# Three conditioning visits begun one block earlier, in buffers taken from the shared ring

## The chip, the core and the metric

The kernel runs on one core of a Trainium2 chip. The metric is the device time of one launch in microseconds. TensorE (PE in the profile) multiplies, ScalarE (ACT) and VectorE (DVE) work element by element, GpSimd (POOL) does small jobs, and SyncE's queue (SP) issues nearly all loads. Each engine runs its own instructions in the order in which they were compiled, and waits for others through semaphores.

## What is computed

One layer of a hybrid decoder for two request groups at once, 256 prompt tokens and 8 x 4 sample tokens, so that every matrix product has 288 columns. Cut to what matters here:

```python
mod = silu(c) @ w_ada + b_ada                      # six parts: sh1, sc1, g1, sh2, sc2, g2, 2048 wide each
h = rmsnorm(x, norm1) * (1 + sc1) + sh1
u_pool, z, xbc, dt = split(h @ w_in)               # 512, 1536, 2560, 24 columns
mix = concat([pool_mixer(u_pool), ssd_mixer(z, xbc, dt)]) @ w_out
x = x + g1 * mix
h2 = rmsnorm(x, norm2) * (1 + sc2) + sh2
up = h2 @ w_up                                     # then a short conv and silu on the gate half
x = x + g2 * (act @ w_down)                        # and a last rmsnorm
```

Parts 0 and 1 of `mod` (sh1, sc1) are needed before `w_in`; parts 2 and 3 (g1, sh2) only after `w_out`. The change concerns when the products for parts 2 and 3 are made.

## The kernel before, in words

All weights come once from DRAM, as one long stream cut into pieces of 128 partitions x up to 1024 columns of fp32 (512 KB), loaded into SBUF by `load` (line 267). A weight piece is split into a rounded high part (ACT, `whi`, line 289) and the rest (DVE, `wlo`, line 291), and each 128x128 tile of it gives three matmuls of 288 columns (`mm3`, lines 303 to 305). The conditioning weights are not split: a piece is the moving operand of matmuls whose stationary operand is `sc_c`, the conditioning vectors (line 372, `adag`, for parts 0 and 1; line 405, `adap`, for the others).

**Blocks.** The x/B/C columns of `w_in` and some others (28 column tiles) are made in seven blocks over groups of rows k (`BLOCKS`, line 45). The blocks numbered 4, 5 and 6 each take all 28 column tiles over four row tiles: k 4 to 7, 8 to 11, 12 to 15. A column tile over four rows is one unit of 12 matmuls; a piece holds two units. The loop at line 1046 runs over blocks, and inside over units `i`. While a block runs, the conditioning for the next rows is made in *group visits* (`next(nxt)`): a visit reads four pieces of parts 0 and 1, and after a group's last visit the next rows are modulated. The list `VIS` (line 48) says behind which units the visits stand: in block 5 behind units 3, 9, 15 and 20.

**The ring.** Pieces for blocks 0 to 5 and for the group visits share a ring of 16 buffers (`_W`, line 494): four tagged `raw` and four tagged `rawa` in the pool `w1`, eight tagged `raw` in the pool `w0`. `_need_order` (line 89) sorts the pieces by an assumed time of need, and `top_up` (line 277) issues them while fewer than 16 (`RAW0 + RAW1 + RAWA`) lie between the next load and the oldest one not yet fetched. Six pieces are loaded before, then 103 in this order, so the last has the number 108.

**Part visits.** Parts 2 and 3 are made by the generator `adas = ada_visits((2, 3), AK)` (lines 412 and 959): 16 visits. Each loads four pieces into the four `rawa` buffers (one step), lets two more steps pass, and in the fourth step runs its matmuls, the last loaded piece first, held at their place in program order. The pieces of the following visit go into the same four buffers, so they are loaded once the matmuls have read them. All 16 visits take 65 steps. Before the change, block 6 (the last) begins with closing `w0`, moving the four `rawa` buffers out of the shared ring, the `dt` product, the small loads of `late_states`, and one step of `adas` (line 1069). Then each unit of block 6 pulls 4 x 5.01/28 = 0.716 step, and each unit of the gate stretch 4 x 11.01/62 = 0.710 step.

**Gate stretch.** After block 6 come eight more column tiles of `w_in` (`uz_units`, line 943: six of z, the gate of the mixer, and two of the pool), 64 units of six matmuls. Between them runs `back` (line 1033), the convolution and the state-space part, which has small matmuls in the midst of ACT and DVE work. At its end `drain(adas)` (line 1105) finishes what visits are left.

The order of each engine's instructions is fixed by a scheduler at compile time: it goes by program order as priority, but may put an instruction whose buffer is free ahead of an earlier one that still waits. Matmuls of the visits keep their place.

Of the kernel before, what the change touches and what calls it, by code (L numbers as in the profile page):

```python
# [39 lines left out]
RAW0, RAW1, RAWA, RAW2 = 8, 4, 4, 4  # L40
# [4 lines left out]
BLOCKS = [((0, 1), (0, 28)), ((1, 1), (0, 16)), ((1, 3), (16, 28)), ((2, 2), (0, 16)),  # L45
          ((4, 4), (0, 28)), ((8, 4), (0, 28)), ((12, 4), (0, 28))]

VIS = ([14], [1, 9], [2, 6, 10], [4], [3, 9, 15, 20], [3, 9, 15, 20], [])
TP = 0.4
TV, TL = 2.0, 2.8  # L50
GB = 4
VA = (5.01 / 28, 11.01 / 62)
AK, AY, ADA_OUT = 2, 2, 4

RB1, RB2, RB3 = 1.0, 1.0, 1.0
# [26 lines left out]
def _xbc_chunks(bi):  # L82
    (k0, gk), (a, b) = BLOCKS[bi]
    mper = RAWC // (gk * P)
    cuts = [a, *([4, 8] if bi == 0 else []), *range(a + (12 if bi == 0 else mper), b, mper), b]
    return [(list(range(k0, k0 + gk)), list(range(m, n))) for m, n in zip(cuts, cuts[1:])]


def _need_order():

    visits = iter([(gi, q) for gi in range(1, len(KGROUPS))
                   for q in range(0, KT * 256 * KGROUPS[gi][1] // RAWC, AQ[gi])])
    t, need = 0.0, []
    for bi, ((_, gk), (a, b)) in enumerate(BLOCKS[:-1]):
        chunks = {ms[0]: ci for ci, (_, ms) in enumerate(_xbc_chunks(bi))}
        for i, m in enumerate(range(a, b)):
            if m in chunks and (bi or chunks[m] > 1):
                need.append((t - TL, ("xbc", bi, chunks[m])))
            t += TP * gk
            if i in VIS[bi]:  # L100
                gi, q = next(visits)
                need += [(t, ("ada", gi, q + j)) for j in range(AQ[gi])]
                t += TV
    assert next(visits, None) is None
    return [key for _, key in sorted(need, key=lambda e: e[0])]
# [59 lines left out]
def kernel(ctx: ExitStack, tc, ins, outs):  # L165
# [99 lines left out]
    wp = [None]  # L265

    def load(key, ring="raw"):
        off, cols = S.items[key]
        t = wp[0].tile([P, RAWC], F32, tag=ring, name="raw_" + "_".join(map(str, key)))
        nc.sync.dma_start(t[:, :cols], wflat[off:off + P * cols].rearrange("(p n) -> p n", p=P))  # L270
        return t

    queue = deque(_need_order())
    ahead = {}
    nloads = [0]

    def top_up():

        while queue and nloads[0] - min((n for n, _ in ahead.values()), default=nloads[0]) < RAW0 + RAW1 + RAWA:
            key = queue.popleft()  # L280
            ahead[key] = (nloads[0], load(key))
            nloads[0] += 1

    def fetch(key):
        return ahead.pop(key)[1]
# [7 lines left out]
    def split(raw, a, n, name, urgent=True, pin=False):  # L293
        with tc.high_priority() if urgent else nullcontext():
            cast, (hi, lo, rest) = split_steps(raw, a, n, name)
        if pin:
            tc.keep_in_program_order(cast)
            tc.keep_in_program_order(rest)
        return hi, lo
# [112 lines left out]
    def ada_visits(parts, step):  # L412

        plan = [(part, k0) for part in parts for k0 in range(0, KT, step)]
        ahead, end = [], None

        def chunks(v):
            part, k0 = plan[v]
            for k in range(k0, k0 + step):
                for h in range(2):  # L420
                    ahead.append((k, h, load(("adap", part, k, h), "rawa")))
            for _ in range(3):
                yield

        yield from chunks(0)
        for v, (part, k0) in enumerate(plan):
            if end:
                ada_end(*end)
                end = None
            if k0 == 0:  # L430
                ps = pa.tile([P, 512], F32, tag="ada", name=f"adap{part}")
            whole(ps, ahead, step, True)
            ahead.clear()
            if k0 + step == KT:
                end = part, ada_sb(ps, 512, f"p{part}")
            yield
            if v + 1 < len(plan):
                yield from chunks(v + 1)
        ada_end(*end)
        yield  # L440
# [137 lines left out]
    def late_loads():  # L578
        nc.vector.tensor_copy(selr, seli)
        nc.vector.tensor_scalar(csr, vec[:, K_TRI:K_TRI + N], 0.0, None, ALU.mult)  # L580

    def late_states():
        nc.sync.dma_start(poolw, ins["pool_w"])
        n = XT * NB * 3
        st = sx[0].tile([P, n + 4 * NB * 15], F32, name="st")
        nc.sync.dma_start(st, ins["st"])
        stc.append(st[:, 0:n].rearrange("p (g m b l) -> p g m b l", g=4, m=5, b=NB))
        nc.gpsimd.tensor_copy(ups.rearrange("p m b l -> p (m b) l")[:, :, 0:15],
                              st[:, n:].rearrange("p (m l) -> p m l", l=15))
# [353 lines left out]
    def uz_units(m):  # L943
        for ps in project_units(("uz", m), KT, order=MIXK if m == ULATE[-1] else None):
            yield
        if m < 4:
            nc.scalar.copy(upp[:, m, 15:15 + NP], ps[:, 0:NP])
            nc.scalar.copy(ups[:, m, :, 15:19], samp(ps[:, NP:N]))
        else:
            g, t = divmod(m - 4, 3)  # L950
            nc.scalar.activation(zy_of(g)[:, t, :], ps[:, :N], AF.Silu)
            zdone.add((g, t))
# [6 lines left out]
    adas = ada_visits((2, 3), AK)  # L959
# [78 lines left out]
    def pull(gn, rate):  # L1038

        credit[id(gn)] = credit.get(id(gn), 0.0) + rate  # L1040
        while credit[id(gn)] >= 1:
            credit[id(gn)] -= 1
            next(gn, None)

    nloads[0] = len(first) + KT // 4
    for bi in range(len(BLOCKS)):
        last = bi + 1 == len(BLOCKS)
        top_up()
        if last:

            wp[0].drop(w0)
            wp[0].move("rawa", "raw", "rawa")
            w0_ctx.close()
            sx[0] = mx_ctx.enter_context(tc.tile_pool(name="sx", bufs=1, reuse_waits="tile"))
            wp[0].add(sx[0], "raw", "raw", 1)
            raw = load(("dt",))[:, :KT * NH].rearrange("p (k h) -> p k h", h=NH)
            wdt = wp[0].tile([P, RAWC], F32R, tag="whi", name="whi_dt")
            with tc.high_priority():
                nc.gpsimd.memset(wdt.bitcast(F32), 0.0)
                both = wdt[:, :DTW * KT].rearrange("p (k c) -> p k c", c=DTW)  # L1060
                nc.scalar.copy(both[:, :, 0:NH], raw)
                nc.vector.tensor_tensor(both[:, :, 32:32 + NH], raw, both[:, :, 0:NH].bitcast(F32), ALU.subtract)
            ps = pm.tile([P, 512], F32, tag="mm", name="mm_dt")
            for k in range(KT):
                w = wdt[:, DTW * k:DTW * k + P]
                nc.tensor.matmul(ps[:, :N], w, xhi[0][k], start=k == 0, stop=False)
                nc.tensor.matmul(ps[:, :N], w, xlo[0][k], start=False, stop=k == KT - 1)
            late_states()
            next(adas)
            dt_stage(ps)  # L1070
        elif bi == 4:
            nc.sync.dma_start(vec, ins["vec"])
        elif bi == 5:
            late_loads()
        for i, m in enumerate(xbc_units(bi)):
            if not last:
                top_up()
                if bi == 0 and i in (3, 7, 13):
                    ci = {3: 2, 7: 3, 13: 4}[i]
                    ready["xbc", 0, ci] = split(fetch(("xbc", 0, ci)), 0, len(_xbc_chunks(0)[ci][1]) * P,  # L1080
                                                f"xbc0_{ci}", pin=True)
                if i in VIS[bi]:
                    next(nxt)
                    top_up()
            else:
                pull(back, 0.5 if m < 20 else RB1) if m >= 9 else None
                pull(adas, 4 * VA[0])

    late = {}
    n = 0  # L1090
    zlast = 3 * (4 - ZEARLY) * KT // YK
    for m in list(range(4 + 3 * ZEARLY, 16)) + ULATE:
        for _ in uz_units(m):
            n += 1
            for gn in late.values():
                pull(gn, 0.5)
            pull(adas, 4 * VA[1])
            pull(back, RB2 if n <= zlast else RB3)
            if n == zlast:
                drain(back)  # L1100
                back = ssd3
        if m < 4:
            late[m] = pool_units(m)
            next(late[m])
    drain(adas)
    wp[0].move("rawa", "rawa", "raw")
    adas = ada_part_units(4, AY)
# [36 lines left out]
    for i in range(KT // YK):  # L1144
# [6 lines left out]
        if i == 3:  # L1151
            psq = aux("ysum")
            col_sums(psq, ssq, ones[:, 0:1], True, True)
            _, rstdy = rstd_of(psq, NH * 64, "rstdy")
# [209 lines left out]
    rstdf, _ = rstd_of(psf, D, "rstdf", False)  # L1364
# [151 lines left out]
```

## Time and profile before

| what | value |
|---|---|
| median of three runs | 1350.02 us (1346.77 to 1351.32) |
| the profiled execution's own time | 1346.89 us |
| its span, first to last instruction | 1345.1 us |
| granted TensorE clock | 0.998 |
| PE busy | 1329.6 us (99%) |
| DVE, ACT, POOL busy | 824.6, 578.6, 222.3 us |
| block 5 | about 133 to 185 us |
| dt and block 6 | about 185 to 252 us |
| gate stretch | about 252 to 364 us |

The profiled execution took 1346.89 us, of which its span holds 1345.1 us; 1.8 us lie around it. It is 3.1 us under the median of the runs. The profile has 512 records of `adap` matmuls in all, 256 of them for the 16 visits of parts 2 and 3, so 16 records stand for one visit. In the tables of stretches the columns are: stretch, its length, busy time of PE, PEld (weight loads), DVE, ACT and POOL (number of instructions), granted clock, busy share of the DMA engines, GB/s. In the timelines they are: start, length, engine, line, operation, output and inputs, shapes, count, and in brackets the idle time before it and what ended that.

### The profile page before, as it was taken

Reading aid. Unit: us, or ns where it says so; the run is one execution under the profiler, and the core shown is the slowest. Engines: PE = TensorE matmul, PEld = TensorE weight load, DVE = VectorE, ACT = ScalarE, POOL = GpSimd, SP = SyncE. Lnnn points to the kernel's source line nnn. Section 1 sums busy time; section 2 is a strip of 40 time slices with the busy share of each in tenths; the row PEclk is TensorE's granted clock in tenths of the full one; section 3 lists DMA queues with packets and bytes.
Section 4 is the critical chain, followed back from the end, with each engine's and each line's share of the span. In section 5 each row is a group of like instructions: output and inputs, shape, how many; then the busy total and the mean of one; then the engine's idle time right before and its main releaser. Section 6 shows DMA issues by size and latency. Waiting matters only on the chain.

```text
span 1345.1 us, 26211 instructions
## 1 busy us (share of the span) xinstructions
PE 1329.6 (99%) x10517; PEld 1245.2 (93%) x10517; DVE 824.6 (61%) x1382; ACT 578.6 (43%) x911; POOL 222.3 (17%) x449
## 2 busy tenths in 40 slices
PE   9999999999999999999999999999999999999997
PEld 7889998876789889989999999999999999999997
DVE  5675569878765468555565445665655556666543
ACT  5343245677733335433443333433433334444442
POOL 0000012123122123100221001221210021122221
PEclk9999999999999999999999999999999999999999
DMA  9999678888898886777455445555545555555521
GB/s 373 405 408 370 232 263 309 316 298 318 299 395 325 311 322 226 270 268 260 171 193 176 166 175 189 198 191 194 182 162 170 189 194 191 191 191 196 184 72 71
DMA packets 97482, 323.19 MB, mean 240 GB/s; under 512 B 10768, under 2 KB 19920, under 8 KB 97360
## 3 DMA queue, kind: packets, MB, share of 16 engines
q1 hardware_dynamic: 93600, 310.79, 63.9%
q0 software_dynamic: 3184, 9.69, 2.0%
q8 instruction: 82, 1.34, 0.4%
q10 hardware_dynamic: 576, 1.03, 0.2%
q14 instruction: 40, 0.33, 0.1%
HBM read 309.78 MB, written 10.39 MB: 238 GB/s over the span
## 4 chain that ended last, share of the span: by engine, by line
PE 93%; DMA 2%; DVE 2%; issue 2%; ACT 0%; POOL 0%; SPq 0%; DVEq 0%; POOLq 0%; ACTq 0%
PE mm_down L304 7%; PE mm_down L303 7%; PE mm_down L305 7%; PE mm_val L304 6%; PE mm_gate L303 6%; PE mm_gate L304 6%; PE mm_gate L305 6%; PE mm_val L305 6%; PE mm_val L303 6%; PE xbc L303 4%; PE xbc L304 4%; PE xbc L305 4%; PE adap L405 4%; PE adag L372 2%; PE mm_out L303 2%; PE mm_out L304 2%
## 5 line engine op out<-in xcount | busy, mean ns | idle before, releaser
L304 PE MATMUL mm_down<-al,whi_down 128*128 128x288 f32 x688 | 202.5, 294 | 0.0
L303 PE MATMUL mm_down<-ah,whi_down 128*128 128x288 f32 x688 | 202.4, 294 | 0.0
L305 PE MATMUL mm_down<-ah,wlo_down 128*128 128x288 f32 x688 | 202.0, 294 | 0.0
L304 PE MATMUL mm_val<-h2l,whi_val 128*128 128x288 f32 x640 | 189.1, 296 | 0.0
L304 PE MATMUL mm_gate<-h2l,whi_gate 128*128 128x288 f32 x640 | 189.0, 295 | 0.0
L303 PE MATMUL mm_gate<-h2h,whi_gate 128*128 128x288 f32 x640 | 188.7, 295 | 0.0
L305 PE MATMUL mm_val<-h2h,wlo_val 128*128 128x288 f32 x640 | 188.4, 294 | 0.0
L305 PE MATMUL mm_gate<-h2h,wlo_gate 128*128 128x288 f32 x640 | 188.3, 294 | 0.0
L303 PE MATMUL mm_val<-h2h,whi_val 128*128 128x288 f32 x640 | 187.9, 294 | 0.0
L291 DVE TENSOR_TENSOR wlo_gate<-raw_gate,whi_gate 128x1024 fp32r<-128x1024 f32 x80 | 99.1, 1238 | 135.6 <-ACT whi_gate L289 135.6
L291 DVE TENSOR_TENSOR wlo_down<-raw_down,whi_down 128x1024 fp32r<-128x1024 f32 x96 | 108.0, 1125 | 116.6 <-ACT whi_down L289 116.6
L289 ACT CAST whi_down<-raw_down 128x1024 fp32r<-128x1024 f32 x96 | 92.4, 962 | 167.1 <-PE mm_down L304 119.3
L289 ACT CAST whi_gate<-raw_gate 128x1024 fp32r<-128x1024 f32 x80 | 84.0, 1051 | 159.5 <-PE mm_gate L304 78.1
L289 ACT CAST whi_val<-raw_val 128x1024 fp32r<-128x1024 f32 x80 | 84.1, 1051 | 127.4 <-issue 111.4
L303 PE MATMUL xbc<-h1h,whi_xbc 128*128 128x288 f32 x448 | 133.5, 301 | 0.8 <-ACT h1h L490 0.7
L304 PE MATMUL xbc<-h1l,whi_xbc 128*128 128x288 f32 x448 | 132.3, 296 | 0.0
L305 PE MATMUL xbc<-h1h,wlo_xbc 128*128 128x288 f32 x448 | 130.1, 295 | 0.0
L303 PEld LDWEIGHTS mm_down<-ah,whi_down 128*128 128x128 f32 x688 | 129.2, 188 | 0.0
L304 PEld LDWEIGHTS mm_down<-al,whi_down 128*128 128x128 f32 x688 | 129.1, 188 | 0.0
L305 PEld LDWEIGHTS mm_down<-ah,wlo_down 128*128 128x128 f32 x688 | 129.0, 188 | 0.0
L303 PEld LDWEIGHTS mm_gate<-h2h,whi_gate 128*128 128x128 f32 x640 | 120.3, 188 | 5.0 <-ACT ah L1279 3.4
L305 PEld LDWEIGHTS mm_gate<-h2h,wlo_gate 128*128 128x128 f32 x640 | 120.5, 188 | 0.0
(331 smaller groups left out, 2979.1 us busy)
## 6 DMA issues: line engine op xcount, KB each, us to landing
raw_adap<-wflat SPq DMA_DIRECT2D x128, 512.0 KB, 6.4
raw_gate<-wflat SPq DMA_DIRECT2D x80, 512.0 KB, 3.6
raw_val<-wflat SPq DMA_DIRECT2D x80, 512.0 KB, 3.5
raw_ada<-wflat SPq DMA_DIRECT2D x64, 512.0 KB, 9.6
raw_xbc<-wflat SPq DMA_DIRECT2D x50, 512.0 KB, 9.5
raw_down<-wflat SPq DMA_DIRECT2D x48, 512.0 KB, 3.4
raw_out<-wflat SPq DMA_DIRECT2D x32, 512.0 KB, 7.3
raw_down<-wflat SPq DMA_DIRECT2D x32, 384.0 KB, 3.4
```

The lines of the kernel that those rows point to most:

```text
L289: yield nc.scalar.copy(hi[:, :n], raw[:, a:a + n])
L291: yield hi, lo, nc.vector.tensor_tensor(lo[:, :n], raw[:, a:a + n], hi[:, :n].bitcast(F32), ALU.subtract)
L303: nc.tensor.matmul(ps, whi[:, w], bh, start=first, stop=False)
L304: nc.tensor.matmul(ps, whi[:, w], bl, start=False, stop=False)
L305: nc.tensor.matmul(ps, wlo[:, w], bh, start=False, stop=last)
L372: i = nc.tensor.matmul(ps[32 * j:32 * j + 32, :nb], sc_c[:, ck, :], raw[:, c:c + nb], start=q0 + n == 0, stop=q0 + AQ[gi] >= nq and n + 1 ...
L405: i = nc.tensor.matmul(ps[32 * j:32 * j + 32, :], sc_c[:, k, :], raw[:, 512 * (j % 2):512 * (j % 2) + 512], start=k == step - 1, stop=k == ...
```

## The change

- The group visits of block 5 stand behind units 1, 5, 9 and 13 (before: 3, 9, 15 and 20). The order of need changes with them.
- At unit 14 of block 5 the four `rawa` buffers leave the shared ring, and the limit in `top_up` falls from 16 to 12. From unit 14 to unit 27 each unit makes one whole step of `adas`: 14 steps, which hold visits 0, 1 and 2 and the loads of visit 3. Their matmuls stand behind units 17, 21 and 25.
- The single step of `adas` ahead of `dt_stage` in block 6 is gone, and so is the move of the buffers there.
- Block 6 pulls 4 x 4.01/28 = 0.573 step a unit (16 steps: visits 3 to 6, and the loads of visit 7), and the gate stretch 4 x 8.76/62 = 0.565 step (35 are left: visits 7 to 15). Before, it was 5 visits in block 6 and 11 in the gate stretch.

```diff
-VIS = ([14], [1, 9], [2, 6, 10], [4], [3, 9, 15, 20], [3, 9, 15, 20], [])
+VIS = ([14], [1, 9], [2, 6, 10], [4], [3, 9, 15, 20], [1, 5, 9, 13], [])
...
-VA = (5.01 / 28, 11.01 / 62)
+VA = (14, 4.01 / 28, 8.76 / 62)
...
+    room = [RAW0 + RAW1 + RAWA]
...
-        while queue and nloads[0] - min((n for n, _ in ahead.values()), default=nloads[0]) < RAW0 + RAW1 + RAWA:
+        while queue and nloads[0] - min((n for n, _ in ahead.values()), default=nloads[0]) < room[0]:
...
             wp[0].drop(w0)
-            wp[0].move("rawa", "raw", "rawa")
             w0_ctx.close()
...
             late_states()
-            next(adas)
             dt_stage(ps)
...
                 if i in VIS[bi]:
                     next(nxt)
                     top_up()
+                if bi == len(BLOCKS) - 2 and i >= VA[0]:
+                    if i == VA[0]:
+                        room[0] -= RAWA
+                        wp[0].move("rawa", "raw", "rawa")
+                    next(adas)
             else:
                 pull(back, 0.5 if m < 20 else RB1) if m >= 9 else None
-                pull(adas, 4 * VA[0])
+                pull(adas, 4 * VA[1])
...
-            pull(adas, 4 * VA[1])
+            pull(adas, 4 * VA[2])
             pull(back, RB2 if n <= zlast else RB3)
```

## The prediction

> **What bounds the kernel now.** I read the page's head first, to see which engine is full.
>
> ```profile
> span 1345.1 us, 26211 instructions
> PE 1329.6 (99%) x10517; PEld 1245.2 (93%) x10517; DVE 824.6 (61%) x1382; ACT 578.6 (43%) x911; POOL 222.3 (17%) x449
> PE 93%; DMA 2%; DVE 2%; issue 2%; ACT 0%; POOL 0%; SPq 0%; DVEq 0%; POOLq 0%; ACTq 0%
> ```
>
> PE is idle for 1345.1 - 1329.6 = 15.5 us in all, and 93% of the chain that ended last is PE. The change neither adds nor removes a matmul, so only idle time of PE can move. The second view is the table of stretches for block 6 and for the gate stretch, the third the waits of PE from block 6 into the output stage.
>
> ```profile
> 185.30:252.40 67.10, 67.04 (x514) 56.87 (x512) 58.28 (x134) 30.24 (x43) 15.43 (x29) 1.00 0.79 289
> 252.40:364.00 111.60, 109.60 (x918) 82.76 (x915) 86.48 (x160) 89.09 (x199) 23.25 (x35) 1.00 0.85 310
> ...
> PE adap L405 <- DMA raw_adap<-wflat: 0.7, 1, 0.7
> PE pool L939 <- DVE pout L933: 0.6, 1, 0.6
> PE y L871 <- DVE e L859: 0.6, 2, 0.4
> ```
>
> Block 6 has 0.06 us of PE idle time, the gate stretch 111.60 - 109.60 = 2.00 us: 0.7 for a part visit whose pieces came late, 1.2 for results of DVE. That is the whole room for a gain in these stretches. A verdict of faster or slower needs more than 0.3%, or 4.05 us (about what a measurement of this kernel can tell from no change; the three runs alone lie 4.55 us apart). Block 5 must now carry three visits more. Its timetable comes from the group visits in it:
>
> ```profile
> 139.20 1.93 PE L372 MATMUL adag<-raw_ada,sc_c 128*32 128x256 f32 x32
> 150.78 1.93 PE L372 MATMUL adag<-raw_ada,sc_c 128*32 128x256 f32 x32
> 162.37 1.93 PE L372 MATMUL adag<-raw_ada,sc_c 128*32 128x256 f32 x32
> 172.37 1.93 PE L372 MATMUL adag<-raw_ada,sc_c 128*32 128x256 f32 x32
> ```
>
> Between the second and the third lie six units (11.59 us), between the third and the fourth five (10.00): a unit takes 1.59 us, a visit 11.59 - 6 x 1.59 = 2.05. Four units stand ahead of the first, so the block began at 139.20 - 4 x 1.59 = 132.84.
>
> **The group visits moved forward.** Behind units 1, 5, 9 and 13 they begin at 132.84 + 2 x 1.59 = 136.02, then every 4 x 1.59 + 2.05 = 8.41 us: 144.43, 152.84, 161.25. Are their pieces there? I follow the order of need through the ring: the four visits read loads 81 to 84, 87 to 90, 93 to 96 and 99 to 102 (before: 82 to 85, 89 to 92, 96 to 99, 102 to 105). A load goes out when the one 16 places earlier has been read.
>
> ```profile
> 111.02 1.75 SPq L270 DMA_DIRECT2D raw_ada<-wflat  x4
> ...
> 120.58 2.49 SPq L270 DMA_DIRECT2D raw_ada<-wflat  x4
> ...
> DMA to landing us min/median/max: 8.6/10.5/10.5
> ```
>
> Places 66 to 68 and 72 to 74, read by the last two group visits of block 4, come free where these two rows stand: 111 and 120.6. The longest landing of group pieces that I found, 10.5 us (third row, those issued at 92 to 98, while DMA was full), gives 123 and 134, with 136.02 and 144.43 as the needs. The later two wait for pieces read by about 136 and 138, so they land by 149, against 152.84 and 161.25. Nothing waits, and I cost this at nothing; its cover is some 10 us in each case. The last modulation comes 11 us sooner and stands beside matmuls, as before.
>
> **The four buffers and the limit.** Followed through `top_up`, load 108 goes out behind unit 10, before and after; at unit 14 the queue is empty, so the lower limit never acts. And SP shows that the four buffers already served part visits there:
>
> ```profile
> 151.48 1.28 SPq L270 DMA_DIRECT2D raw_xbc<-wflat  x3
> 163.07 0.33 SPq L270 DMA_DIRECT2D raw_dt<-wflat  x1
> 163.45 0.42 SPq L583 DMA_DIRECT2D poolw<-pool_w  x1
> 163.97 1.04 SPq L270 DMA_DIRECT2D raw_adap<-wflat  x2
> 165.11 1.13 SPq L270 DMA_DIRECT2D raw_xbc<-wflat  x2
> 173.93 0.80 SPq L270 DMA_DIRECT2D raw_adap<-wflat  x2
> 174.79 0.42 SPq L270 DMA_DIRECT2D raw_xbc<-wflat  x1
> 175.26 0.96 SPq L759 DMA_DIRECT2D h<-h  x2
> ```
>
> Visit 0 was loaded at 164 to 174, in block 5, though its matmuls came later. Cost of this part: 0. What is new on SP is that 12 more loads (visits 1 to 3) may stand ahead of block 6's pieces and the state loads `h`. The scheduler let block 6's loads pass waiting ones here (rows 165.11 against 173.93), and their buffers now come free with the group visit at 152.84, 10 us sooner than that of the `dt` row at 163.07. I cost it at 0 for block 6; POOL's queue is not passed by anything.
>
> **Three part visits in block 5.** This is the term that decides. Visit 0 stands four units behind the last group visit, visits 1 and 2 four units behind the one before, so each begins 8.41 us after the start of the visit that frees its buffers: 169.66, 178.07, 186.48. How soon can four pieces be there?
>
> ```profile
> 346.36 1.92 PE L405 MATMUL adap<-raw_adap,sc_c 128*32 128x512 f32 x16
> ...
> L270 SPq DMA_DIRECT2D raw_adap<-wflat x4: 328/368/422, 347.5 to 348.8; - x4
> DMA to landing us min/median/max: 3.5/5.8/8.2
> ...
> 357.02 1.92 PE L405 MATMUL adap<-raw_adap,sc_c 128*32 128x512 f32 x16
> ...
> L270 SPq DMA_DIRECT2D raw_adap<-wflat x4: 328/369/422, 358.1 to 359.4; - x4
> DMA to landing us min/median/max: 3.8/5.0/6.3
> ...
> 367.07 1.92 PE L405 MATMUL adap<-raw_adap,sc_c 128*32 128x512 f32 x16
> ```
>
> The visit at 357.02 had its next pieces issued from 358.1 to 359.4 with little beside them; the last landed at most 6.3 us after its issue, at 365.7, which is 8.7 us after the visit began. The one at 346.36, with other weights in the queue, got its last at 348.8 + 8.2 = 357.0, or 10.65 us after. Against 8.41 a visit in block 5 is 0.3 us late in the first case and 2.25 in the second. Before, visits stood some 10 us apart. The last loaded piece is read first, so lateness goes straight into PE, and the unit behind it waits too.
>
> Which row is nearest? These rows say how full DMA is:
>
> ```profile
> 100.00:110.00 10.00, 10.00 (x84) 9.66 (x87) 4.31 (x11) 2.67 (x3) 0.00 (x0) 1.00 1.03 410
> ...
> 152.00:162.00 10.00, 10.00 (x86) 9.50 (x78) 5.61 (x8) 2.10 (x2) 0.00 (x0) 1.00 0.64 235
> 162.00:172.00 10.00, 10.00 (x94) 8.91 (x93) 4.80 (x8) 3.15 (x3) 0.00 (x0) 1.00 0.70 244
> ```
>
> At 410 GB/s a visit's 2.10 MB take 5.1 us of each 8.41, which leaves 3.3 us, or 1.35 MB, for others. In the way come two `h` loads (1.18 MB), released earlier by the modulation, and a piece or two of block 6 (0.52 MB each): enough to delay one visit of three. So visits 0 and 2 at 0.3 each and visit 1 half-way, at 1.3: +1.9 us. Ends: 0 (block 5 has no PE idle time to give back) and 3 x 2.25 = 6.75.
>
> The Trainium skill, page "DMA: Bandwidth & Descriptors", section "Anatomy of one DMA — SWDGE (gpsimd) path", gives a DMA about 2.0 us plus its bytes over 436 GB/s. That is a fit for GpSimd's path; as an estimate, 2.10 MB would then be there 6.8 us after the first issue, 7.9 after the visit's start, no visit would be late, and the sum would be 1.9 us less. The trace's 358.1 to 365.7 is 7.6 us, so the measurement speaks for lateness; this is rival C.
>
> **Block 6 and the gate stretch.** Block 6 gets 4 visits for 5, the gate stretch 9 for 11. Visits in the gate stretch now stand 4/0.565 = 7.1 units apart in place of 5.6, so (367.07 - 357.02 - 2.05) x 7.1/5.6 + 2.05 = 12.2 us, more than the 10.65 above: the 0.7 us wait for pieces goes. What is late next is DVE, because visits are PE work behind which DVE catches up:
>
> ```profile
> 230.00:240.00 10.00, 10.00 (x80) 8.40 (x79) 9.95 (x23) 4.92 (x5) 4.07 (x6) 1.00 0.83 296
> 240.00:250.00 10.00, 10.00 (x74) 7.87 (x73) 9.90 (x18) 4.26 (x6) 3.58 (x5) 1.00 0.69 261
> ...
> 331.94 1.58 DVE pp L922
> ...
> 360.79 1.14 DVE wlo_out L291
> ```
>
> DVE is full in 230 to 250, yet block 6 as a whole needs 58.28 us of it in 67.10 - 2.05 = 65.05, so its backlog runs off behind it. In the gate stretch the chain of waits goes through DVE around these two rows, at 324 to 337 and 357 to 363, some 20 us. PE's cover thins there by 2 x 2.05 / 111.6 = 3.7%, or 0.7 us. Ends: -1.2 (those waits vanish) and +4.1 (all of the cover becomes waiting).
>
> **Sum.** +1.9 - 0.7 + 0.7 = +1.9 us. Against the profiled execution's 1346.89 that is 1348.8; against the median, 3.1 us higher, 1352.
>
> **The rivals.**
>
> *A, slower: every one of the three visits comes late.* If the `h` loads, `st` and block 6's pieces fall in the queue ahead of each of them, as at 346.36, block 5 loses 6.75 us; with -0.7 and +0.7 that is 1356.8. For it: four loads of 512 KB and others share one queue, and the spacing of 8.41 is below every start-to-landing time above. Against it: DMA was only 0.64 to 0.70 busy in 152 to 172. It decides from a mean lateness of 4.05/3 = 1.35 us.
>
> *B, slower: DVE takes over in the gate stretch.* All of the 4.1 us of cover becomes waiting: 1.9 - 0.7 + 4.1 = 5.3, or 1355.3. For it: 58.28 of 67.10 us in block 6, then 86.48 of 111.6. Against it: PE waited 1.2 us for DVE in all.
>
> *C, a little faster: the visits in block 5 are hidden.* If the buffers' older readers let the first loads out sooner, nothing is late there; the 0.7 goes, and half of the DVE waits at best: -1.3, or 1348.7. For it: only 0.3 us is missing. Even with all 2.0 us of idle time gone it isn't 0.3%.
>
> That the buffers' move does nothing by itself is part of the sum already.
>
> **How the numbers follow.** Forecast 0.45, A 0.25, B 0.10, C 0.20. The range runs from C with its last waits gone (1350.02 - 2.0 = 1348.0, and 1 us for the scatter of the runs) to A and 1 us more: 1347 to 1358. The likeliest case alone: 1350 to 1354. Slower by over 0.3%: A and B, 0.35. Faster: no mechanism, only the scatter of the medians, 0.06. Within: 0.59.
>
> **What would show it.** In the changed kernel: group visits about 136, 144, 153 and 161; `adap` visits about 170, 178 and 186, with PE waits on `raw_adap` of 0 to 2 us each (A: 2 and more, C: none); `mm_dt` some 6 us later than before; no wait for `raw_adap` in the gate stretch; its length near 107.5 us, and waits on DVE near 2 us (B: 4 or more). The prediction is wrong if block 6's first pieces land late behind the visits' loads on SP, if group visits wait for their pieces, or if the gate stretch doesn't shrink by the two visits.

## The result, and the profile after

| | before | after |
|---|---|---|
| median, 11 runs each on one chip | 1348.19 us (1346.77 to 1351.32) | 1351.43 us (1350.69 to 1354.11) |
| ratio, 95% interval | 1 | 1.0026 (1.0018 to 1.0033) |
| profiled execution, its span | 1346.89, 1345.1 us | 1351.43, 1349.7 us |

The change costs 0.26% of 1348.19, or 3.5 us (the two medians lie 3.2 us apart). That is inside the 0.3% that I called a measurement's limit, and with eleven runs on each side it is clearly above zero. The forecast was +1.9 us. The two profiled executions, which the rest compares, lie 4.6 us apart in span: that of before is 1.3 us under the median of its runs, that of after stands on its own. So differences of about a microsecond between two profiles can be scatter.

The head of the page of the changed kernel, for comparison with the three lines of before:

```profile
span 1349.7 us, 26220 instructions
PE 1331.4 (99%) x10517; PEld 1246.2 (92%) x10517; DVE 822.4 (61%) x1382; ACT 581.9 (43%) x913; POOL 221.5 (16%) x449
PE 94%; DVE 2%; DMA 2%; ACT 1%; issue 1%; POOL 0%; SPq 0%; DVEq 0%; POOLq 0%
```

The same 10517 matmuls, and PE still fills 99%. Its idle time went from 15.5 us to 1349.7 - 1331.4 = 18.3. To place the 4.6 us I cut both executions at the same events (first matmul of `mm_dt`, `uz`, `mm_out` and `mm_up`). First the stretches of before, cut at these events (dt with block 6, the gate stretch, and the output stage up to the first matmul of `mm_up`), in the columns of the prediction's tables:

```profile
185.70:252.40 66.70, 66.64 (x511) 56.47 (x509) 58.28 (x134) 30.24 (x43) 15.43 (x29) 1.00 0.80 290
252.40:362.40 110.00, 108.09 (x910) 81.59 (x907) 84.88 (x155) 87.49 (x195) 23.25 (x35) 1.00 0.84 309
362.40:493.60 131.20, 130.73 (x997) 111.76 (x995) 74.15 (x146) 46.08 (x67) 30.08 (x57) 1.00 0.88 334
```

And the same view of the kernel after: dt with block 6, the gate stretch, the output stage.

```profile
189.90:258.40 68.50, 66.91 (x510) 56.41 (x508) 57.74 (x132) 30.66 (x43) 11.50 (x27) 1.00 0.85 323
258.40:367.70 109.30, 107.01 (x894) 81.73 (x891) 82.38 (x157) 89.80 (x197) 25.90 (x38) 1.00 0.79 290
367.70:499.30 131.60, 129.22 (x981) 111.41 (x979) 77.48 (x149) 47.84 (x67) 32.01 (x57) 1.00 0.85 322
```

| stretch | part visits, before to after | length before | length after | difference |
|---|---|---|---|---|
| start to `mm_dt` | 0 to 2 | 185.7 | 189.9 | +4.2 |
| dt and block 6 | 5 to 5 | 66.7 | 68.5 | +1.8 |
| gate stretch | 10 to 9 | 110.0 | 109.3 | -0.7 |
| output stage | 1 to 0 | 131.2 | 131.6 | +0.4 |
| from `mm_up` to the end | | 851.5 | 850.4 | -1.1 |

Read the table by its second column, which counts where the visits were found. Before, the sixteenth visit stood in the output stage (at 367.07), so the gate stretch held ten and not the eleven named ahead of the prediction. Two visits of 2.05 us went ahead of `mm_dt`, which is 4.1 us late for it. One visit each left the gate stretch and the output stage, which should have become 2.05 us shorter each. The last cut falls into the waits for `h2h`, 1.2 us in both kernels: before, 0.8 us of them lie behind the cut, after, none. With these 0.8 us put on one side, the last two differences are -0.4 and -0.3. So the two stretches gave back 0.7 and 0.4 us of 2.05 each: the work was paid for in front and hardly given back behind. From `mm_dt` to the end it is 1159.4 us before and 1159.8 after, with two visits less.

A part of the reason is in the waits of PE from block 5 to the output stage of the kernel after (us in total, times, longest):

```profile
PE xbc L304 <- DVE cvp L712: 1.6, 2, 1.3
...
PE pool L940 <- DVE pout L934: 1.1, 2, 0.9
PE cse L852 <- DVE yo L838: 1.0, 1, 1.0
PE mm_out L304 <- ACT whi_out L290: 1.0, 2, 0.8
PE y L872 <- DVE e L860: 0.3, 1, 0.3
```

No wait on `raw_adap` is left in this stretch, and none for the pieces of the moved visits. All that is there is PE waiting for results of DVE and ACT: 5.0 us, where before had 0.6 + 0.6 for DVE and 0.7 for pieces. With the waits at `mm_up`, PE's idle time from 130 to 520 us grew from 3.27 to 6.25 us, +3.0. The rest of the 4.6 us lies in PE's busy time (1329.6 to 1331.4 with the same matmuls), which no run here takes apart. In the gate stretch it is the larger part: PE's idle time grew by 0.4 us there, while its busy time fell by 1.1 us for a visit of 1.9. How far one pair of profiles carries is seen from the first experiment below: its kernel is as fast as before, and its profile has 4.62 us of idle time in the same window.

Where the visits came to stand is in the timeline of PE of the kernel after (start, length, ..., count):

```profile
136.15 1.93 PE L373 MATMUL adag<-raw_ada,sc_c 128*32 128x256 f32 x32
...
161.39 1.93 PE L373 MATMUL adag<-raw_ada,sc_c 128*32 128x256 f32 x32
...
175.70 1.93 PE L406 MATMUL adap<-raw_adap,sc_c 128*32 128x512 f32 x16
...
185.18 1.92 PE L406 MATMUL adap<-raw_adap,sc_c 128*32 128x512 f32 x16
...
189.92 0.29 PE L1066 MATMUL mm_dt<-h1h,whi_dt 128*128 128x288 f32 x1
...
194.92 1.92 PE L406 MATMUL adap<-raw_adap,sc_c 128*32 128x512 f32 x16
```

The four group visits stand within 0.2 us of the predicted places. The part visits do not: not at 169.66, 178.07 and 186.48, but at 175.70, 185.18, and 194.92, the third behind `mm_dt`. Nothing waits in front of them. In the compiled order of PE the first of them stands 7.6 units behind the last group visit, where the program has it 4 behind, and the third 0.4 units behind `mm_dt`. So the scheduler deferred them at compile time; that matmuls of the visits keep their place, as the text ahead of the prediction has it, does not hold against the matmuls around them. It also shifted the later ones: in units of 12 matmuls behind `mm_dt`, the visits of block 6 and the next stand at 5, 10, 16, 21, 27 before and at 0.4, 4.4, 11, 18, 25 after. SyncE's queue in the kernel after shows when pieces were asked for:

```profile
162.09 1.75 SPq L270 DMA_DIRECT2D raw_adap<-wflat  x4
163.89 0.49 SPq L270 DMA_DIRECT2D raw_dt<-wflat  x1
...
176.79 1.75 SPq L270 DMA_DIRECT2D raw_adap<-wflat  x4
...
186.28 1.75 SPq L270 DMA_DIRECT2D raw_adap<-wflat  x4
...
221.57 1.64 SPq L760 DMA_DIRECT2D h<-h  x3
```

The second and third sets of four go out 1.1 us after the start of the visit that frees the buffers, and the visits stand 9.48 and 9.74 us apart: between the 8.7 and the 10.65 that the prediction had measured from start to landing, and more than the 8.41 of the program's order. The `h` loads, which the prediction put in the way of the second visit, go out at 221.57 and later, so they stood in the way of none; before, the first two went out at 175.26. PE waits for none of them in either kernel.

### The profile page after: what moved, and what is told of

Read it like the earlier page. It is cut to its first block, busy times and chain, and to the rows that moved or that the text cites. A ratio compares the mean times of both kernels' runs of the same rounds, so it can differ in the third digit from the quotient of the medians.

```text
span 1349.7 us, 26220 instructions
## 1 busy us (share of the span) xinstructions
PE 1331.4 (99%) x10517; PEld 1246.2 (92%) x10517; DVE 822.4 (61%) x1382; ACT 581.9 (43%) x913; POOL 221.5 (16%) x449
## 4 chain that ended last, share of the span: by engine, by line
PE 94%; DVE 2%; DMA 2%; ACT 1%; issue 1%; POOL 0%; SPq 0%; DVEq 0%; POOLq 0%
PE mm_down L305 7%; PE mm_down L304 7%; PE mm_down L306 7%; PE mm_val L305 6%; PE mm_gate L304 6%; PE mm_gate L305 6%; PE mm_gate L306 6%; PE mm_val L306 6%; PE mm_val L304 6%; PE xbc L304 4%; PE xbc L305 4%; PE xbc L306 4%; PE adap L406 4%; PE adag L373 2%; PE mm_out L304 2%; PE mm_out L305 2%
## 5 line engine op out<-in xcount | busy, mean ns | idle before, releaser
L292 DVE TENSOR_TENSOR wlo_down<-raw_down,whi_down 128x1024 fp32r<-128x1024 f32 x96 | 107.5, 1120 | 116.8 <-ACT whi_down L290 116.6
```

What stands on the lines that cost most here:

```text
L292: yield hi, lo, nc.vector.tensor_tensor(lo[:, :n], raw[:, a:a + n], hi[:, :n].bitcast(F32), ALU.subtract)
```

## The experiments

These accounts of the 3.5 us were tried, and the letters stand in the expectations (S was put down last, behind the run with denser visits):

- **T, thinned cover.** Visits are PE work behind which DVE and ACT catch up. Behind `mm_dt` they cost almost nothing, ahead of it their full 2 us.
- **P, the place in block 6.** The loss is the 1.3 us wait behind the reciprocal of `dt`, which a visit no longer covers.
- **G, the group visits** moved forward cost by themselves.
- **F, full price.** PE work counts in full wherever it stands, so that the loss has some other cause.
- **S, a matter of which visits.** Only certain ones are cover, and others would give their time back.

Two more letters stand in the expectations. L says that block 6's own pieces come late; but the kernel after has no wait of PE for a weight split of block 6, only the two for `cvp` above. D says that DVE time as such is missing beside the reciprocal.

### The group visits alone

```diff
-VIS = ([14], [1, 9], [2, 6, 10], [4], [3, 9, 15, 20], [3, 9, 15, 20], [])
+VIS = ([14], [1, 9], [2, 6, 10], [4], [3, 9, 15, 20], [1, 5, 9, 13], [])
```

> The kernel before with the group visits of block 5 behind units 1, 5, 9 and 13 and nothing else of the change. Theory P (the loss of 0.26% comes from where the part visits now stand in block 6 and later, measured against DVE work): 1.000 of before, within 0.05%; block 5 keeps its length of about 52.8 us. Rival G (the early group visits cost something themselves, through pieces that come late or a modulation that falls into the splits): 0.05% to 0.2% slower, with waits of PE in block 5.

Measured: 1.0002 (0.9993 to 1.0011) of the kernel before. `mm_dt` begins at 185.4 (before: 185.7). The group visits moved forward cost nothing, and G is out. Behind block 5 its profile has longer waits than that of before all the same (1.5 us for pieces in place of 0.7, and 0.5 for `yo`), at an equal time.

### The reciprocal of dt made cheap, in both kernels

The lines of the kernel after in question are these of DVE's timeline; the add into `cvp` at 203.49, which releases PE's matmul at 204.03 after 1.30 us of waiting, stands behind the reciprocal and a weight split:

```profile
200.12 1.94 DVE L612 RECIPROCAL dttmp<-dttmp 24x288 f32<-24x288 f32 x1
201.99 1.15 DVE L292 TENSOR_TENSOR wlo_xbc<-raw_xbc,whi_xbc 128x1024 fp32r<-128x1024 f32 x1
...
203.49 0.40 DVE L712 TENSOR_TENSOR cvp<-cvp,xbc 128x256 f32<-128x256 f32 x1
```

Before, the reciprocal ran from 196.36 to 198.30 (DVE), and a visit's 1.92 us stood at 197.93 (PE), at its end, while DVE did the split behind it:

```profile
196.36 1.94 DVE L611 RECIPROCAL dttmp<-dttmp 24x288 f32<-24x288 f32 x1
...
197.93 1.92 PE L405 MATMUL adap<-raw_adap,sc_c 128*32 128x512 f32 x16
```

```diff
-        nc.vector.reciprocal(z[:, :N], z[:, :N])
+        nc.vector.tensor_scalar(z[:, :N], z[:, :N], -0.1, 0.6, ALU.mult, ALU.add)
```

In the kernel before:

> The kernel before, with the reciprocal of the dt stage (DVE, 1.94 us) put in place by a linear form of some 0.3 us, so dt and all that follows from it is not computed right. Theory P: a part visit covers the reciprocal in the kernel before, so nothing is gained: within 0.05%. Rival D (DVE time as such is what the stretch lacks): 1.6 us, or 0.12%, faster.

In the kernel after:

> The changed kernel with the same cheap form. Theory P: the wait of 1.3 us on DVE beside the reciprocal goes, so 1.3 to 1.8 us less than the changed kernel, which leaves about 1.7 to 2.2 us (0.13% to 0.16%) over before. Rival L (block 6's pieces come late behind the visits' loads): the wait stays, 0.26% over before.

Measured: 0.9996 (0.9987 to 1.0005) and 1.0024 (1.0015 to 1.0033). The wait that P blames is gone from the second, and its time is what it was. Its waits of PE over the same stretch:

```profile
PE pool L940 <- DVE pout L934: 2.0, 2, 1.2
PE adap L406 <- DMA raw_adap<-wflat: 1.5, 2, 1.0
...
PE mm_out L304 <- ACT whi_out L290: 0.8, 2, 0.6
```

The `cvp` wait of 1.3 us went, `pool` grew from 1.1 to 2.0, and 1.5 us for pieces came in. P fell. D had 1.6 us for the kernel before; its medians differ by 0.5.

### Block 6's visits back at the places of before

The kernel after, with block 6's rate of before and one visit less begun in block 5, so that two visits stand ahead of `mm_dt` as in the kernel after, and five in block 6 at 5, 10, 16, 21 and 27 as before.

```diff
-VA = (14, 4.01 / 28, 8.76 / 62)
+VA = (14, 5.01 / 28, 8.76 / 62)
...
-                    next(adas)
+                    if i < 23:
+                        next(adas)
```

> The changed kernel, but visits 0 and 1 alone stand in block 5, and in block 6 visits 2 to 6 take the places behind dt (5, 10, 16, 21 and 27 units) that visits 0 to 4 had before; 2 fewer are left for the gate stretch and behind. Theory P: block 6 loses its 1.5 us of idle time, mm_uz starts 4.2 us later than before and not 6.0; the whole is about 2 us (0.15%) over before. Rival T (each visit taken out of the gate stretch costs about 1.2 us there, wherever the others stand): block 6 as in P, but 2.4 us or more lost in the gate stretch and the output stage, 0.2% and more over before. Rival L: block 6 keeps a wait of over 1 us.

Measured: 1.0025 (1.0015 to 1.0035), the same as the whole change. Its stretches, dt with block 6, the gate stretch, and eight microseconds of the output stage:

```profile
190.00:256.90 66.90, 66.67 (x510) 56.47 (x508) 58.20 (x134) 30.18 (x43) 15.44 (x29) 1.00 0.87 324
256.90:365.20 108.30, 104.96 (x878) 81.25 (x875) 85.41 (x150) 85.58 (x191) 25.05 (x35) 1.00 0.79 290
...
368.00:376.00 8.00, 6.61 (x37) 3.22 (x36) 6.30 (x18) 2.71 (x7) 1.34 (x5) 0.79 0.56 188
```

Block 6 loses nothing here (66.90 us, 0.23 idle). The gate stretch is 108.3 us with 3.3 us idle (before: 1.9), the first `mm_up` comes at 501.2 (after: 499.3), and the total is no better; the third row has PE idle for 1.4 us and the granted clock at 0.79. The profiled execution took 1353.15 us, 1.7 over the median of 1351.50, so its waits may be longer than usual. Most of them:

```profile
PE pool L940 <- DVE pout L934: 2.9, 2, 1.5
PE cse L852 <- DVE yo L838: 1.1, 1, 1.1
```

So the loss is not tied to where block 6's visits stand. Repaired in one stretch, it turns up in the next two, though how it divides between them is read from this one execution. This is for T and a second time against P.

### Three visits without their matmuls: gate stretch and output stage

If T holds, PE work taken out of the gate stretch saves nothing; by F it saves all of its 3 x 2.05 us. In the kernel before, three of its visits issue no matmuls, their loads stay:

```diff
-            whole(ps, ahead, step, True)
+            if v not in (9, 11, 13):
+                whole(ps, ahead, step, True)
```

> The kernel before, with the matmuls of visits 9, 11 and 13 (all in the gate stretch) left out, their loads kept; so part 3 is not computed right. The two kernels with other places in block 6 lost as much as the change, so theory P has fallen. Theory T (from dt to the output stage the length is set by DVE and ACT work, and visits there are cover that costs PE nothing): PE saves 3 x 2.05 = 6.15 us of work, the time falls by 2 us (0.15%) or less. Rival F (a visit costs its full PE time wherever it stands, and the loss is in queues and loads): 5 to 6 us (0.4%) faster.

And the control, three visits of part 4 in the output stage, where DVE has 74.15 us in 131.20:

```diff
-            whole(ps, [(k, h, load(("adap", part, k, h))) for k in range(k0, k0 + ay) for h in range(2)], ay, False)
+            chunks = [(k, h, load(("adap", part, k, h))) for k in range(k0, k0 + ay) for h in range(2)]
+            if part == 5 or k0 not in (4, 6, 8):
+                whole(ps, chunks, ay, False)
```

> The control: the kernel before, with the matmuls of three visits of part 4, in the output stage, left out, their loads kept; so part 4 is not computed right. Both theories: the output stage is PE's alone, 5.5 to 6.2 us (0.41% to 0.46%) faster. If it too gains less than 2 us, visits are cheap everywhere and theory T says nothing about the gate stretch.

Measured: 0.9997 (0.9988 to 1.0006) for the gate stretch, 0.9969 (0.9957 to 0.9981) for the output stage. The same amount of PE work gives some 0.3 us in the one and 4.1 us in the other. F is out for the gate stretch, and the 5.5 us and more that both theories had for the output stage were missed. The other visits keep their places in the program; compiled, those behind the first one left out stand about a unit sooner. So this tests mainly the number of visits. Its waits in the gate stretch of the first:

```profile
PE y L872 <- DVE e L860: 2.0, 2, 1.8
PE mm_uz L305 <- DVE wlo_uz L291: 1.2, 1, 1.2
PE cse L852 <- DVE yo L838: 0.9, 1, 0.9
...
PE bt L795 <- DVE xde L790: 0.6, 1, 0.6
```

and the stretches around the longest one, eight microseconds before it and eight from it on:

```profile
252.60:363.40 110.80, 105.84 (x863) 82.56 (x860) 81.47 (x153) 86.79 (x194) 23.96 (x35) 0.97 0.85 311
...
316.00:324.00 8.00, 6.37 (x55) 5.46 (x53) 5.86 (x15) 7.45 (x16) 1.73 (x3) 1.00 1.01 402
324.00:332.00 8.00, 7.03 (x37) 4.68 (x41) 4.70 (x11) 2.30 (x7) 2.81 (x4) 0.57 0.90 353
```

PE waits 5.0 us in 110.8 instead of 1.9 in 110.0, and the granted clock falls to 0.57 for eight of them: about 8 x 0.43 = 3.4 us of full-speed PE time. Both together eat the 6.15 us. So in this profile, with a mean clock of 0.995, the missing gain is partly waiting and partly a slower clock behind a wait. The clock is not all of it: four of the eleven runs had a mean clock of 0.997, as runs of before mostly have 0.997 or 0.998, and took 1347.78 to 1348.67 us, only 0.3 to 1.2 us under the median of before, 1348.97. In the control a part of the gain goes into waits:

```profile
PE mm_out L305 <- DVE wlo_out L291: 1.9, 3, 0.7
PE mm_out L303 <- ACT whi_out L289: 1.3, 2, 0.6
```

The kernel before waits for neither `wlo_out` nor `whi_out`. The control's profiled execution took 1346.61 us, 1.8 over the median of its runs, 1344.85, so the usual waits may be shorter.

### Three others in the gate stretch, and three in block 6

```diff
-            whole(ps, ahead, step, True)
+            if v not in (5, 6, 10):
+                whole(ps, ahead, step, True)
```

> The kernel before with the matmuls of visits 5, 6 and 10 left out (three others of the gate stretch, two of them at its begin), their loads kept, so parts 2 and 3 are not computed right. e10 moved visits within the gate stretch, took none out and lost 0.18%, so the place of a visit counts too. Theory T (anywhere in the gate stretch a visit is cover): 2 us (0.15%) faster or less, as with visits 9, 11 and 13. Theory S (it is single places that are cheap, those of 9, 11 and 13 by chance): 4 us (0.3%) faster or more.

The same with `(1, 2, 3)`, visits of block 6:

> The kernel before with the matmuls of visits 1, 2 and 3 left out, all in block 6, their loads kept, so part 2 is not computed right. Block 6 has 58.3 us of DVE work in 67.1 us. If cover is needed there too: 2 us (0.15%) faster or less. If DVE's backlog runs off into the gate stretch, as the prediction had it, part of the 6.15 us is saved in block 6 and given back as waits behind it: mm_uz starts 3 us or more earlier, the whole gains less than that.

Measured: 1.0007 (0.9998 to 1.0016), so three other visits of the gate stretch left out gain nothing either: T, not S. Waits of that kernel that the one before does not have, and then the table of its stretches from 316 us:

```profile
PE xt L788 <- ACT ec L858: 2.0, 2, 1.6
PE mm_uz L305 <- DVE wlo_uz L291: 1.7, 1, 1.7
...
PE xt L788 <- ACT cf L744: 1.0, 1, 1.0
```

```profile
316.00:320.00 4.00, 1.39 (x8) 0.71 (x8) 2.03 (x5) 3.97 (x11) 0.40 (x2) 0.95 1.03 406
320.00:328.00 8.00, 6.77 (x44) 4.77 (x44) 7.05 (x12) 2.05 (x3) 1.87 (x3) 0.60 0.28 107
```

ACT now ends waits too: it is busy 3.97 of the four microseconds from 316, PE 1.39, and behind that the clock is down to 0.60 for eight. All eleven runs had a mean clock of 0.993 to 0.995, so the runs do not part the two causes here; in the profile the idle time alone takes most of it, 7.1 us in the gate stretch for 1.9 before. For block 6: 0.9975 (0.9966 to 0.9985), 3.4 us of 6.15 gained, at a mean clock as before. Its block 6 is 64.5 us with 61.71 us of PE, against 66.70 and 66.64:

```profile
185.70:250.20 64.50, 61.71 (x462) 55.14 (x460) 55.77 (x129) 30.37 (x43) 12.27 (x27) 1.00 0.82 305
```

Removed work of 6.15 us made block 6 some 2.2 us shorter (the first `uz` at 250.2 for 252.4), where I had expected 3 and more. By the times alone, a little under half of the visits' work gave nothing back there, nearly all of it in the gate stretch (a slower clock included), a third of it in the output stage.

### One visit moved in place of two

```diff
-VA = (14, 4.01 / 28, 8.76 / 62)
+VA = (14, 5.01 / 28, 9.76 / 62)
...
-                    next(adas)
+                    if i < 19:
+                        next(adas)
```

> The changed kernel, but only visit 0 stands in block 5; visits 1 to 5 take the places that visits 0 to 4 had behind dt, and the rest are spread over the gate stretch, so that all 16 are over ahead of the output stage. Theory T: one visit (2.05 us) is moved out of the stretch in which it covers DVE work, dt starts 2.1 us later, and the stretch from dt on gets shorter by 0 to 1 us: 1.1 to 2.1 us (0.08% to 0.16%) over before. If a visit were saved at its full price behind dt (rival F): within 0.03% of before. If the loss came with the move as such (buffers, loads): 0.2% and more, as with two.

Measured: 1.0011 (1.0002 to 1.0020), medians 1.0 us apart. `mm_dt` begins at 188.0, 2.3 us late for one visit, and PE waits 2.2 us for `pout` and 1.3 us for `yo` (before: 0.6 and none). The loss grows with the number of visits moved, as T has it. But the visit moved came out of the output stage: the gate stretch holds ten visits as before, spaced otherwise, and is longer all the same.

```profile
254.60:367.00 112.40, 109.28 (x917) 82.72 (x913) 86.40 (x165) 89.47 (x200) 24.80 (x35) 1.00 0.80 297
```

Some 0.6 us of this row is the end of the visits' work, which before stands behind the cut. Gate stretch and output stage together, from the first `uz` to the first `mm_up` with its wait, are the firmer figure: 242.0 us with eleven visits before (241.2 and the 0.8 put on one side), 241.7 with ten here, 240.9 with nine in the kernel after. At its full price each visit less would be worth 2.05 us.

### The other direction: more visits in the gate stretch

```diff
-VA = (5.01 / 28, 11.01 / 62)
+VA = (5.01 / 28, 12.01 / 62)
```

> The kernel before with more steps to a unit in the gate stretch (4 x 12.01/62 in place of 4 x 11.01/62), so that visits stand closer together and the last of the 16 moves from half-way into the first output tile to its start: the other direction of the change. Theory T: cover is put where DVE is late, so at most the 2 us of idle time there can go: 0 to 0.08% faster than before. The opposite, 0.05% and more slower, would come from pieces that land too late for the closer visits.

Measured: 1.0018 (1.0009 to 1.0027), slower, where T alone had it level or faster. The sixteenth visit stays in the output stage (0.3 units behind the first `mm_out`, before 2.3), so what this changed is mainly the visits' places between the units. PE's waits:

```profile
PE adap L405 <- DMA raw_adap<-wflat: 1.2, 2, 0.8
...
PE cse L851 <- DVE yo L837: 1.0, 1, 1.0
PE pool L939 <- DVE pout L933: 1.0, 3, 0.5
```

Visits wait longer for pieces (1.2 us in place of 0.7), and the waits for `yo` and `pout` grew by 1.4 us. So the number of visits is not all: their places count for 2.4 us by the medians here, and T as it stood was too simple. That these waits are the way in which they count is argued, since the profile of the group visits alone has waits as long at no loss. The change altered number and places at once, and no run on it parts them: how much of its loss is due to the new spacing stays open.

### Less DVE work in block 6, in both kernels

If DVE is what runs late, the two kernels should come together when DVE has less to do. The convolution keeps one of its three further taps:

```diff
-            for i in range(1, 4):
+            for i in range(1, 2):
```

In the kernel before:

> The kernel before, with two of the three multiply-adds of the width-4 conv left out (40 DVE instructions of about 0.5 us between block 6 and the gate stretch), so the mixer's x/B/C are not computed right. Theory T: before is near balance between PE and DVE, so it gains its 2 us of idle time at most: 0.05% to 0.15% faster. Rival A (ACT, not DVE, sets the length): no gain.

In the kernel after:

> The changed kernel with the same two multiply-adds left out. Theory T with DVE as the limit: PE is the limit again and the two visits moved ahead of dt are saved behind it, so it comes within 1 us (0.08%) of the lightened kernel before. Rival A (ACT sets the length) or rival F: it stays 2.5 us or more (0.2%) over the lightened kernel before.

Measured: 0.9990 (0.9981 to 0.9999) and 1.0005 (0.9996 to 1.0014). The gap between the two fell from 0.26% to 0.15%, by the medians (1348.15 and 1348.95) from 3.2 us to 0.8. I had expected 0.08% or less. The gap became smaller, as it should if DVE's work is a part of the limit, but the intervals of the two ratios overlap, and the step from 0.26% to 0.15% is smaller than the width of either: this speaks for DVE and does not show it. In the profile of the second, a wait of 2.6 us for `whi_out` of ACT ends in its output stage at 383.45, with the clock at 0.79 behind it:

```profile
384.00:392.00 8.00, 7.71 (x44) 7.25 (x44) 6.19 (x13) 3.14 (x5) 2.37 (x5) 0.79 0.99 368
```

That execution took 1353.42 us, 4.5 over the median of 1348.95, so it shows what can happen where ACT is late, and not what usually does.

No version that computes the whole layer beat the kernel before.

## Why the prediction was right and wrong

**Size and sign.** Forecast +1.9 us and within 0.3%, measured +3.5 us and within 0.3%; 1351.43 is inside the likeliest case's own range, 1350 to 1354. The time was right for largely wrong reasons, and in part by luck: the 1352 started from 1350.02, the median of three runs, which is 1.8 us above that of eleven, and this made up for a change that was put some 1.5 us too small. By one of its own signs the prediction is wrong: the gate stretch did not shrink by two visits, to near 107.5 us, but by 0.7 us to 109.3.

**Group visits at no cost: right.** Predicted at 136.02 to 161.25, found at 136.15 to 161.39 with no wait, and alone they cost 0.02% with zero well inside the interval. The cover of "some 10 us in each case" was 6 and not 10 for the third visit by the prediction's own figures (136 + 10.5 against 152.84), which changed nothing.

**Buffers and limit at no cost: nothing speaks against it.** The first four loads go out at 162.09, ahead of `raw_dt` at 163.89, and block 6's pieces came in time. No run tried the limit alone.

**Three part visits late for +1.9 us: wrong, and the step failed at its premise.** The visits were taken to be held behind units 17, 21 and 25, and lateness followed from 8.41 us of spacing. The scheduler moved them apart by 9.48 us and more, so no visit waited, and one of three left block 5. The `h` loads that were to delay the second visit were not in the queue then. What block 5 paid instead was the work itself, 2 x 2.05 us. That alone would have been neutral had the stretches behind become shorter by as much. That the deferral follows from the scheduler's own estimate of the loads is likely, since the spacing it chose fits the measured landings; it was not tried.

**The 0.7 us wait for pieces in the gate stretch goes: right.** It is gone.

**DVE waits grow by 0.7 us: the mis-sized term.** In the profiles PE's waits for DVE grew from 1.2 to 4.0 us and those for ACT, the ones at `mm_up` aside, from none to 1.0, so this term should have been near +3.8; with the 0.7 gained, PE's idle time grew by 3.0 us. Up to 1.4 us of this may be scatter between profiles. The mechanism is rival B's, cover that becomes waiting, but B placed all of it in the gate stretch and on DVE. The idle time is 1.6 us in block 6 (before: 0.06), 2.3 in the gate stretch with one visit less (before: 1.9), and 1.1 in the first part of the output stage (before: none), and ACT ended most of the waits of that last part. Taking a share of PE's work (3.7%) times some 20 us where the chain runs through DVE was the error: it prices lost cover at 17% of its 4.1 us. With three visits out, the gate stretch gave back 0.3 of 6.15 us, and 1.2 at most in runs at the usual clock, so most of the cover is lost there, not a sixth of it. How the loss behind `mm_dt` divides between fewer visits, their new places and a busier PE stays open.

**Block 6's backlog "runs off behind it": wrong.** 58.28 us of DVE in 65.05 left room on average. A visit had stood at the end of the 1.94 us reciprocal, and without one there PE waited 1.3 us. With three visits less in it, block 6 itself became 2.2 us shorter and not 6.15. Repairing the place of the reciprocal left the time as it was, so the average was no argument either way.

**A** (late pieces) did not occur, since no visit waited. **C** (hidden, a little faster) was excluded by the interval. Its condition, that no visit in block 5 is late, came true, but it did not count the visits' own 2 x 2.05 us, and its idea that the DVE waits could halve went the wrong way.

## What to carry to other kernels

An engine that is 99% busy is not one whose work counts in full: in a stretch where two other engines are some 80% busy each and hand it small results, filler work can be cover. Before filler is moved out of such a stretch, take some of it away there and see what the time does; here three fillers out saved 0.3 us in one stretch and 4.1 us in another. And read the compiled order before reasoning from the order in the program, because a scheduler may defer work whose loads it thinks late.

## What the runs showed of the hardware

**The granted clock fell behind short waits.** In the kernel with three visits less in the gate stretch, a wait of PE of 1.85 us ended at 324.37, and the clock was 0.57 from 324 to 332. With the three others, PE was busy 1.39 us of the four from 316 to 320, and the clock was 0.60 from 320 to 328. The kernel with block 6's places restored had 0.79 from 368 to 376, around a wait of 1.39 us that ended at 369.73. The 1.30 us wait at 204 in the kernel after had no such effect, nor had one of 1.8 us for a piece in the kernel before with the light convolution. The Trainium skill, page "TensorE: Matmul & The Clock Gate", section "Part 1: The HAM clock gate (the "warmup" mystery)", has the clock halved after an idle window of some 3.4 us. No single wait here was that long: waits of 1.4 to 2.6 us, or several in four microseconds, came before the drops, so by these rows the measurement differs and decides. Why one wait has the effect and another does not stays open.

**The clock goes with the runs' scatter.** Of the eleven runs of the kernel after, three had a mean clock of 0.996 and took 1353.62 to 1354.11 us; the other eight had 0.997 or 0.998 and took 1350.69 to 1352.04. That a drop behind a wait makes this difference of 2.5 us is argued, since none of the three has a profile. One case bears it out: of the kernel after with the light convolution, the one run of eleven at 0.996 is the profiled one, and it has the wait of 2.6 us, the 0.79 behind it and a time 4.5 us over the median. None of the prediction's terms had such a cost.
